# Gates, branch products and output projection in token form, and three of the gates' four column blocks from seven block products

## The chip, the cores and the metric

One core of a Trainium2 chip runs the whole kernel in one launch. The metric is the device time of that launch in microseconds, the median of several runs. All matrix products are done on TensorE in float32r, a float32 format in which one product of full accuracy is made from three passes: each operand is split into a high part and a remainder, and high by high, high by remainder and remainder by high are summed.

## What is computed

A decoder block for 256 tokens and 2048 channels: an mLSTM branch and an attention branch side by side, merged by sigmoid gates, an output projection with a residual, and then a squared-ReLU MLP with a residual. What the change touches is the middle of it:

```python
mq, mk, mv, mo, mi, mf, aq, ak, av, g_m, g_a = split_cols(rmsnorm(x) @ w_in)
h_m = mlstm(...) * sigmoid(mo)          # 256 x 1024
h_a = attention(...)                    # 256 x 1024
y_m, y_a = h_m @ w_branch_m, h_a @ w_branch_a           # 256 x 2048 each
merged = sigmoid(g_m) * y_m + sigmoid(g_a) * y_a        # g_m, g_a: 256 x 2048 each
x = x + rmsnorm(merged @ w_out)         # w_out: 2048 x 2048
u = square(relu(rmsnorm(x) @ w_up))
x = x + rmsnorm(u @ w_down)
```

## The kernel before, in words

Weights come from HBM in units of 1 MB (128 partitions by 2048 numbers), through three `raw` buffers, on the queue of SyncE (SP). `split` (line 157) turns each unit into high parts (`whi`, a cast on ScalarE, line 169) and remainders (`wlo`, a subtraction on VectorE, line 170), in pieces of 1024 columns with four buffers of each, so about one unit is being used while the next is made. The list `steps` holds for each unit what is loaded, the matmuls and what follows them; the main loop at the end loads and splits step i and then issues matmuls and follow-up of step i-1. A planner then orders each engine's instructions by a model of the time, with the program's order as priority, so it can pull later steps forward; only instructions marked `keep_in_program_order` keep their places.

There are four ways to do the matmuls of a unit. In the feature form (`mm_feat`, lines 188 and 189) the weights are the stationary operand and the 256 tokens stream past: for each of 16 blocks one pass of 512 columns (both parts of the activations) and one of 256. `mm_feat_one` (lines 215 to 217) does the same with three passes of 256. In the token form (`mm_tok`, lines 200 to 205) the activations are stationary and 512 columns of weights stream past: 24 passes of 512 columns for a unit. `mm_factor` (lines 226 to 232) is the token form for 128 tokens: 12 passes of 512 columns.

The order before: the values and mLSTM gate inputs (`av`), the attention heads with `q`, `k` and `mv`, then the mLSTM heads (`mq`, `mk`) with lighter units between them (`mv`, `mo`, the first gate units), then for each of 16 feature blocks c a branch step `br` and the gate steps `gm`, `ga` of block c + 4, then 16 units of the output projection (`wo`), then the MLP. The gates (32 units), `mo` (8), the branches (16) and 15 of the 16 `wo` units are in feature form. Their results come out feature by token; `both` (lines 236 to 241) adds the two halves of the accumulator on ScalarE and VectorE. `mlstm_out` gates and stores the last step of an mLSTM head. After the last `wo` unit (in the form of `mm_feat_one`) `last_mix` forms the norm's factor, `residual` makes the new x and its two parts, and the first up-projection step works on four units at once. `open_mlp` transposes x back into token order on TensorE (line 745).

The MLP already multiplies by seven block products in place of eight: `factors` and `group` make sums of blocks of activations and weights, and a group of seven products goes through `mm_factor`, between steps of the up-projection. Two of the seven weight blocks per group come from adding on VectorE (lines 856, 862 and 878, over 2048 columns) and one from a DMA that adds to what is in its destination (line 871, issued on GpSimd's queue, POOL).

## Time and profile before

| | us |
|---|---|
| median of 3 runs | 1439.17 (1438.96 to 1439.21) |
| the profiled execution's own time | 1440.65 |
| its span, first to last instruction | 1438.9 |
| TensorE matmul (PE) busy in it | 1415.9 |
| VectorE (DVE) busy | 1148.0 |
| ScalarE (ACT) busy | 816.2 |
| mean granted clock of TensorE | 0.998 |

The profiled execution took 1.48 us longer than the median; 1.75 us of its time lie outside its span. Busy time of PE counts a matmul from its start to its modelled end, and consecutive matmuls overlap, so how fast TensorE goes is read from the distance between starts, not from the busy time or the length of one.

### The profile page before, as it was taken

To read this page: it belongs to the slowest core of one execution; us is meant where nothing else is said; L and a number is where in the kernel's file an instruction comes from. 1 tells how busy PE (TensorE), PEld (TensorE's weight loads), DVE (VectorE), ACT (ScalarE), POOL (GpSimd) and SP (SyncE) were. 2 spreads that over 40 slices of the span, in tenths; PEclk is the share of its full clock that TensorE was granted. 3 is DMA by queue.
4 is the path that set the end of the run, shared out by engine and by line. 5 is a ranking of instruction groups with operands and counts; after the bars stand their busy time and mean duration, and the time that the engine had idled before them with its cause. 6 is when DMAs were issued, how large, how long until landed. Compare 5 with 4: busy or idle time off the path is not lost.

```text
span 1438.9 us, 21795 instructions
## 1 busy us (share of the span) xinstructions
PE 1415.9 (98%) x8578; PEld 1253.8 (87%) x8578; DVE 1148.0 (80%) x1607; ACT 816.2 (57%) x1200; POOL 14.5 (1%) x26
## 2 busy tenths in 40 slices
PE   9999999999999999999999999999999999999997
PEld 7888888888888888888899989989889898888975
DVE  7777766776676666665687899898999989999985
ACT  7655465565555444455656565564655655565561
POOL 0000000000000000000000000000000000000000
PEclk9999999999999999999999999999999999999999
DMA  8644444444445545555627665657646667665651
GB/s 258 218 176 176 174 165 161 175 174 176 176 176 182 200 177 195 184 183 197 236 76 247 236 216 179 253 197 263 226 151 242 219 217 239 212 205 193 237 202 59
DMA packets 44167, 281.65 MB, mean 196 GB/s; under 512 B 5024, under 2 KB 7328, under 8 KB 11424
## 3 DMA queue, kind: packets, MB, share of 16 engines
q1 hardware_dynamic: 41904, 265.57, 49.6%
q0 software_dynamic: 2016, 14.68, 5.5%
q8 instruction: 67, 1.10, 0.3%
q14 instruction: 36, 0.29, 0.1%
q10 hardware_dynamic: 144, 0.01, 0.0%
HBM read 278.14 MB, written 2.10 MB: 195 GB/s over the span
## 4 chain that ended last, share of the span: by engine, by line
PE 85%; DVE 11%; issue 2%; ACT 1%; DMA 1%; SPq 0%; DVEq 0%; ACTq 0%
PE acc L188 27%; PE acc L189 14%; PE acc L217 7%; PE acc L215 7%; PE acc L216 7%; DVE wlo L170 6%; PE acc L232 5%; PE acc L226 5%; PE acc L230 5%; PE acc L200 2%; PE acc L205 2%; PE acc L204 2%; DVE xs L774 1%; DVE rawl L862 1%; ACT whi L169 1%
## 5 line engine op out<-in xcount | busy, mean ns | idle before, releaser
L169 ACT CAST whi<-raw 128x1024 fp32r<-128x1024 f32 (+2 forms) x420 | 425.3, 1017 | 420.1 <-PE acc L188 179.1
L170 DVE TENSOR_TENSOR wlo<-raw,whi 128x1024 fp32r<-128x1024 f32 (+2 forms) x420 | 495.0, 1181 | 208.4 <-ACT whi L169 198.0
L188 PE MATMUL acc<-xw,whi 128*128 128x512 f32 x1152 | 408.9, 395 | 0.0
L189 PE MATMUL acc<-xw,wlo 128*128 128x256 f32 x1152 | 328.6, 285 | 0.0
L217 PE MATMUL acc<-hw,wlo 128*128 128x256 f32 x992 | 279.9, 283 | 4.9 <-DVE wlo L170 4.9
L216 PE MATMUL acc<-hw,whi 128*128 128x256 f32 x992 | 279.2, 282 | 0.0
L215 PE MATMUL acc<-hw,whi 128*128 128x256 f32 x992 | 277.7, 282 | 0.0
L188 PEld LDWEIGHTS acc<-xw,whi 128*128 128x128 f32 x1152 | 216.4, 188 | 50.3 <-issue 2.1
L169 ACT CAST whi<-rawl 128x1024 fp32r<-128x1024 f32 x168 | 173.5, 1048 | 116.8 <-PE acc L216 52.2
L189 PEld LDWEIGHTS acc<-xw,wlo 128*128 128x128 f32 x1152 | 216.7, 188 | 0.9
L170 DVE TENSOR_TENSOR wlo<-rawl,whi 128x1024 fp32r<-128x1024 f32 x168 | 201.8, 1218 | 8.4 <-ACT whi L169 6.5
L217 PEld LDWEIGHTS acc<-hw,wlo 128*128 128x128 f32 x992 | 186.9, 188 | 9.9 <-DVE wlo L170 7.3
L215 PEld LDWEIGHTS acc<-hw,whi 128*128 128x128 f32 x992 | 186.0, 188 | 4.6 <-DVE t L757 0.2
L216 PEld LDWEIGHTS acc<-hw,whi 128*128 128x128 f32 x992 | 186.8, 188 | 2.0
L226 PE MATMUL acc<-whi,xs 128*128 128x512 f32 x440 | 174.8, 397 | 2.9 <-ACT whi L169 2.9
L232 PE MATMUL acc<-wlo,xs 128*128 128x512 f32 x440 | 172.4, 397 | 1.8 <-DVE wlo L170 1.8
L230 PE MATMUL acc<-whi,xs 128*128 128x512 f32 x440 | 173.7, 395 | 0.0
L232 PEld LDWEIGHTS acc<-wlo,xs 128*128 128x128 f32 x440 | 82.6, 188 | 21.0 <-DVE wlo L170 4.5
L226 PEld LDWEIGHTS acc<-whi,xs 128*128 128x128 f32 x440 | 82.7, 188 | 20.7 <-ACT whi L169 6.0
L230 PEld LDWEIGHTS acc<-whi,xs 128*128 128x128 f32 x440 | 82.7, 188 | 18.1
L188 PE MATMUL acc<-mg,whi 128*128 128x512 f32 x240 | 84.2, 393 | 0.0
L189 PE MATMUL acc<-mg,wlo 128*128 128x256 f32 x240 | 67.7, 283 | 0.0
(258 smaller groups left out, 1622.1 us busy)
## 6 DMA issues: line engine op xcount, KB each, us to landing
raw<-in_wi_dram SPq DMA_DIRECT2D x96, 1024.0 KB, 4.8
raw<-in_wu_dram SPq DMA_DIRECT2D x64, 1024.0 KB, 6.2
rawl<-in_wd_dram SPq DMA_DIRECT2D x42, 1024.0 KB, 7.8
raw<-in_wd_dram SPq DMA_DIRECT2D x22, 1024.0 KB, 4.9
raw<-in_wo_dram SPq DMA_DIRECT2D x16, 1024.0 KB, 4.8
rawl<-in_wd_dram POOLq DMA_DIRECT2D x14, 1024.0 KB, 10.7
raw<-in_wa_dram SPq DMA_DIRECT2D x8, 520.0 KB, 4.6
raw<-in_wa_dram SPq DMA_DIRECT2D x16, 256.0 KB, 4.7
```

Source lines behind the costliest of these rows:

```text
L169: S.copy(out=hi[:, s], in_=r)
L170: V.tensor_tensor(out=lo[:, s], in0=r, in1=hi[:, s].bitcast(F32), op=ALU.subtract)
L188: PE.matmul(out=accs[i][:, 0:2 * T], lhsT=hi, rhs=m, start=k == 0, stop=False)
L189: PE.matmul(out=accs[i][:, 0:T], lhsT=lo, rhs=m[:, 0, :], start=False, stop=k == nk - 1)
L200: first = PE.matmul(out=acc, lhsT=m[:, 0, ts], rhs=hi, start=start and k == 0, stop=False)
L204: PE.matmul(out=acc, lhsT=m[:, 1, ts], rhs=hi, start=False, stop=False)
L215: PE.matmul(out=acc, lhsT=hi, rhs=m[:, 0, :], start=k == 0, stop=False)
L216: PE.matmul(out=acc, lhsT=hi, rhs=m[:, 1, :], start=False, stop=False)
L217: PE.matmul(out=acc, lhsT=lo, rhs=m[:, 0, :], start=False, stop=k == KT - 1)
L226: first = PE.matmul(out=acc, lhsT=f[:, k, 0], rhs=hi, start=start and k == 0, stop=False, skip_group_check=more)
L230: PE.matmul(out=acc, lhsT=f[:, k, 1], rhs=hi, start=False, stop=False, skip_group_check=more)
L232: PE.matmul(out=acc, lhsT=f[:, k, 0], rhs=lo, start=False, stop=stop and k == 3, skip_group_check=more)
```

## The change

The gates, `mo`, the branch products and the output projection go from feature form to token form. Of the gates' four blocks of 512 columns, the first is done plainly in token form. For each of the other three, the product of 2 x 2 blocks (rows: the two halves of the tokens; inner: the two halves of the 2048 channels; columns: the `ga` and the `gm` block) is made from seven products, each of two steps of `mm_factor`, 14 steps. Four sums of blocks of the activations are made once (`x_scale` and `x_sums` in place in x during the attention heads, and split in `open_gates`), the sums of weight blocks per column block: t by an adding DMA and two additions on VectorE, z by a load and an adding DMA. Per column block 12 units are fetched in place of 8, four of them by adding DMAs on POOL's queue. `mixed` lays plain steps (the last plain gate, the branches) between the 14. Gate results are taken from PSUM by one tanh (plain) or by a few copies and additions (seven products). `merged` transposes the merged activations on TensorE, 32 transposes of 128 columns. The output projection ends in two halves of 128 tokens, and `residual(h)` works on one half at a time, with transposes of the new x; the transposes of `open_mlp` and the matmuls of the squares of x are gone. x is not kept: it is loaded again (`x1_load`, 3 MB with the norm's weights) after the first `wo` unit. The first step of the up-projection has two units in place of four. Buffers move: x, the blocks t and two of the MLP's weight blocks share two places (`k8`), several others share six (`g4`), and `rawl` has two buffers in place of four.

```diff
-    light = [("mv", 1, u) for u in range(4)] + [("mo", c) for c in range(8)]
-    light += [("gm", 0), ("ga", 0), ("gm", 1), ("ga", 1)]
+    light = [("mv", 1, u) for u in range(4)] + [("mo", b, u) for b in range(2) for u in range(4)]
     for h in range(MH):
         for j, n in enumerate(("mq", "mq", "mk", "mk")):
-            o += [(n, 2 * h + j % 2), light[4 * h + j]]
-    o += [("gm", 2), ("ga", 2), ("gm", 3), ("ga", 3)]
-    for c in range(KT):
-        o.append(("br", c))
...
+            o.append((n, 2 * h + j % 2))
+            if j < 3:
+                o.append(light.pop(0))
...
+    def open_gates():
+        pb.close()
+        f = pool["f"] = pb.enter_context(tc.tile_pool(name="pg", bufs=1))
+        for name, src in (("q5", a22), ("q7", a21), ("p6", a11), ("q3", a12)) if SGATES else ():
+            t = fx[name] = f.tile([P, 8, 2, P], F32R, name="fac", tag="fac", bufs=4)
+            S.copy(out=t[:, :, 0], in_=src)
+            V.tensor_tensor(out=t[:, :, 1], in0=src, in1=t[:, :, 0].bitcast(F32),
+                            op=ALU.subtract)
...
+        def load_z(u):
+            r["z", u] = pool["f"].tile([P, 2048], F32, name="z", tag="z", bufs=1)
+            nc.sync.dma_start(out=r["z", u], in_=w(1, 0, u))
+            nc.gpsimd.dma_start(out=r["z", u], in_=w(1, 1, u), accum_op=ALU.add)
...
+        def w_p1(u):
+            t = r["t", u] = k8("t")
+            nc.sync.dma_start(out=t, in_=w(0, 0, u))
+            parts = split(t)
+            nc.gpsimd.dma_start(out=t, in_=w(1, 0, u), accum_op=ALU.add)
+            if u == 0:
+                load_z(0)
+            return parts
+        def w_p6(u):
+            r["22"] = load(w(1, 1, u))
+            if u == 0:
+                load_z(1)
+            add(r["t", u], r["22"])
+            return split(r["t", u])
+        def w_p2(u):
+            raw = load(w(0, 1, u))
+            parts = split(raw)
+            add(r["t", u], raw)
+            return parts
...
+        return [step(n, u) for n, u in (
+            ("p1", 0), ("p1", 1), ("q5", 0), ("q7", 0), ("p6", 0), ("q3", 0), ("q5", 1),
+            ("p6", 1), ("q3", 1), ("q7", 1), ("p2", 0), ("q4", 0), ("p2", 1), ("q4", 1))]
...
+    gate_steps(0, "m")
+    i = len(steps)
+    for k, f in ((i - 3, lambda: mlstm_out(3, heads.pop(3))), (i - 2, open_gates)):
+        src, mm, post = steps[k]
+        steps[k] = src, mm, lambda post=post, f=f: (post(), f())
+    both_gates(1, (gate_steps, 0, "a"))
+    both_gates(2, (branch_steps, 0, "a"), (branch_steps, 0, "m"), (branch_steps, 1, "a"))
+    both_gates(3, (branch_steps, 1, "m"), (branch_steps, 2, "a"), (branch_steps, 2, "m"))
+    then(lambda: [merged(c) for c in range(3)])
...
+        def mm(units):
+            late["hw"] = pa.tile([P, KT, 2, T], F32R, name="hw", tag="xw")
+            late["acc"] = tok_acc["o", 3]
+            for h in range(2):
+                for i in range(2):
+                    mm_tok(late["acc"], units[i], mgmov, 8 + 4 * i, False, i == 1, halves=(h,))
+                if h == 0:
+                    residual(0)
+        def post():
+            keep_warm(8)
+            residual(1)
+            open_mlp()
```

## Rows read from the trace of the kernel before

**Rows 1.** The page: busy time of TensorE, and the chain that ended last, by engine.
```profile
PE 1415.9 (98%) x8578; PEld 1253.8 (87%) x8578; DVE 1148.0 (80%) x1607; ACT 816.2 (57%) x1200; POOL 14.5 (1%) x26
PE 85%; DVE 11%; issue 2%; ACT 1%; DMA 1%; SPq 0%; DVEq 0%; ACTq 0%
```
**Rows 2.** Stretches: length, busy us of PE PEld DVE ACT POOL; clock, DMA share, GB/s.
```profile
440.00:680.00 240.00, 240.00 (x1369) 210.31 (x1368) 156.57 (x226) 122.77 (x194) 0.00 (x0) 1.00 0.51 187
943.50:1030.50 87.00, 85.60 (x553) 77.03 (x552) 81.97 (x84) 51.33 (x60) 1.71 (x2) 1.00 0.62 217
```
**Rows 3.** PE's timeline (start, us, what, [idle before]): 16 blocks in feature form.
```profile
300.10 0.40 PE L188 MATMUL acc<-xw,whi 128*128 128x512 f32 x1
...
305.72 0.39 PE L188 MATMUL acc<-xw,whi 128*128 128x512 f32 x1
```
**Rows 4.** Timeline of PE: 24 passes in token form, first and what follows them.
```profile
198.87 0.40 PE L200 MATMUL acc<-whi,xw 128*128 128x512 f32 x1
...
204.45 0.39 PE L188 MATMUL acc<-xw,whi 128*128 128x512 f32 x1
```
**Rows 5.** Timeline of PE: 38 passes of block products, then 48 of 256 columns.
```profile
1025.64 0.40 PE L226 MATMUL acc<-whi,xs 128*128 128x512 f32 x1
...
1034.28 0.39 PE L232 MATMUL acc<-wlo,xs 128*128 128x512 f32 x1
...
1000.09 0.28 PE L215 MATMUL acc<-hw,whi 128*128 128x256 f32 x1
...
1005.79 0.40 PE L226 MATMUL acc<-whi,xs 128*128 128x512 f32 x1
```
**Rows 6.** Timeline of DVE in the MLP and at the residual: back-to-back instructions.
```profile
944.55 1.22 DVE L170 TENSOR_TENSOR wlo<-raw,whi 128x1024 fp32r<-128x1024 f32 x1
945.68 0.68 DVE L846 TENSOR_TENSOR y<-y,acc 128x512 f32<-128x512 f32 x1
946.28 0.68 DVE L789 TENSOR_TENSOR s_b<-s_a,u 128x512 f32<-128x512 f32 x1
...
959.98 2.28 DVE L862 TENSOR_TENSOR rawl<-rawl 128x2048 f32<-128x2048 f32 x1
962.18 0.68 DVE L846 TENSOR_TENSOR y<-y,acc 128x512 f32<-128x512 f32 x1
...
722.46 0.48 DVE L710 SCALAR_TENSOR_TENSOR hw<-x,sm_in,hw 128x256 fp32r<-128x256 f32 x1
```
**Rows 7.** Timeline of PE and DVE: end of `wo`, first up, transposes, the tail.
```profile
715.82 0.28 PE L217 MATMUL acc<-mg,wlo 128*128 128x256 f32 x1
...
722.77 0.48 PE L215 MATMUL acc<-hw,whi 128*128 128x256 f32 x2
...
754.57 1.47 PE L745 MATMUL sm<-ident,x 128*128 128x128 f32 x12
...
1429.02 0.40 PE L232 MATMUL acc<-wlo,xs 128*128 128x512 f32 x1
...
1432.26 2.08 DVE L979 SCALAR_TENSOR_TENSOR x<-y,f_r,x 128x512 f32<-128x512 f32 x3
```
**Rows 8.** DMA: queues of the page, landing of adding DMAs, their issue, plain loads.
```profile
q1 hardware_dynamic: 41904, 265.57, 49.6%
q0 software_dynamic: 2016, 14.68, 5.5%
...
DMA to landing us min/median/max: 8.2/10.7/14.0
...
1025.94 0.85 POOL L871 DMA_DIRECT2D rawl<-in_wd_dram  x1 [43.08 <-DVE rawl L856]
...
raw<-in_wi_dram SPq DMA_DIRECT2D x96, 1024.0 KB, 4.8
```
**Rows 9.** Timeline of DVE: the last mLSTM head, first step after its keys and last.
```profile
372.30 0.75 DVE L240 TENSOR_TENSOR t<-acc,t 128x256 f32<-128x256 f32 x2
...
408.59 0.41 DVE L246 SCALAR_TENSOR_TENSOR hm<-t,hm 128x256 fp32r<-128x256 f32 x1
```

465 lines of the change are left out of this document (281 added, 184 removed).

## Prediction

> **What bounds the kernel now.** I read the page first: TensorE is busy in 98% of the span, and the chain that ended last runs through it for 85%, with VectorE next at 11% [rows 1]. The reader is to see that this is a TensorE kernel, and that busy time can't tell how much of it is waste. So next I looked at stretches: in 240 us of gates and branches PE is busy all the time at granted clock 1.00, with VectorE busy for 157 us of 240; in one cycle of the MLP VectorE is busy for 82 of 87 us and PE has its first idle time [rows 2]. The gates stage therefore has one limit, the rate at which passes go through TensorE, with VectorE as the next engine in line; the MLP shows what happens when VectorE is nearly full.
>
> The rate comes from starts. A unit in feature form takes 305.72 - 300.10 = 5.62 us [rows 3]; in token form 24 passes take 204.45 - 198.87 = 5.58 us [rows 4]; 37 pitches of block products take 8.64 us, 0.2335 us a pass, and a unit in three passes of 256 columns takes 5.70 us [rows 5]. Per column the four forms agree within 2.2%, so a pass saved is time saved, while a change of form is worth nearly nothing. The chip's notes point the other way here, in two sentences that nothing below needs. The Trainium skill (TensorE: Matmul & The Clock Gate, "Back-to-back issue gap") gives a sustained 131 ns for a pass of 512 columns and 81 ns for one of 128, which would make wide passes much cheaper per column and the token form a gain by itself; the rows have 232 to 234 ns for 512 columns and 119 ns for 256, proportional to columns within 2%, so by the trace there is no such gain.
>
> **The change part by part.**
>
> *Seven products for eight.* Three column blocks, each 8 units of 5.62 us before (44.96 us) and 14 steps of 12 passes after: 168 x 0.2335 = 39.23 us. That is 5.73 us each, **-17.2 us**, on the engine that sets the end.
>
> *Token form of the rest.* 8 gate units, 8 of `mo`, 16 of the branches and 15 of `wo` save 0.04 us each, and the last `wo` unit goes from 5.70 to 5.58: **-2.0 us**.
>
> *Transposes of the merged activations.* They are new: 32 at 0.109 us, from 12 in 1.31 us (the first start to the last one's end, less the first one's fill of 0.16) [rows 7], **+3.5 us**. The gaps that they could fill are counted below.
>
> *End of `wo` to first up-projection.* Before, the last pass of `wo` starts at 715.82 and takes its 0.12, and the first up pass starts at 722.77: 6.8 us without product; then 32 transposes, 3.5 us: 10.3 us. After, count from the end of the first half's 24 passes; the second half's last 5.6 us. The norm's factor needs 2.8 us, as in the tail where the last pass ends at 1429.42 and the first use of the factor starts at 1432.26 [rows 7]. Then VectorE has 4 updates of 512 columns (pitch 0.60) and 16 remainders of 128 columns. The trace has those only at 256 columns, where one lasts 0.48, pitch 0.40 with the overlap of 0.08 that the additions show; halving the columns takes off at most half and at least nothing; remainder and addition of 256 and 512 columns last 0.48 and 0.68, so 128 columns are about 0.10 to 0.13, and I take 0.27 [rows 6]: 2.4 + 4.3 = 6.7 us, done at 9.5. The second half's factor is there by 5.6 + 2.8 = 8.4, so VectorE sets it: one update, four transposes, a cast and a remainder more (0.60 + 0.44 + 0.5 + 0.1, the cast by the row of the 256-column remainder beside it) and the first up pass starts at 11.1. PE lacks 11.1 - 5.6 = 5.5 us, in which 20 of the 32 transposes of the new x lie; 12 follow, 1.3 us. So 6.8 against 10.3: **-3.5 us**. Its ends: 0 (every remainder at 0.40 adds 2, and the planner delays the second factor by one MLP-like queue), and -6 (the first up passes start as the 6.7 us queue of the second half begins, with transposes all hidden). I take the middle since both ends need something the rows don't show. After the start VectorE makes four k in 0.60 + 4 x 0.27 = 1.7 us and two units use four k in 24 x 0.119 = 2.9 us, so PE leads from there; before, with four units, it was close to even.
>
> The sum of these is **-19.2 us**. What could take it back is stalls, which the trace of before doesn't show for this stage; I bound them.
>
> *VectorE in the seven-product stretches.* A 1024-column remainder costs 1.13 us of VectorE, an addition of 512 columns 0.60, of 2048 columns 2.20 [rows 6]. Per column block: 28 x 1.13 + 4 x 2.20 + 6 x 0.60 = 44.0 us, against 39.2 of PE; alone, that is over. The plain units laid between have 2.26 us of VectorE in 5.58 of PE. Block 1 with 4 units: 53.1 of 61.6 us; blocks 2 and 3 with 6 units and 8 or 10 branch additions: 62.4 or 63.6 of 72.7. So 86 to 87%, less than the MLP's 94%, where a cycle of 14 block steps and 8 units should take 168 x 0.2335 + 8 x 5.70 = 84.8 us and takes 87.0 [rows 2, 5]: 2.2 us lost. That row is nearest, and bounds this at 0 to 2.2 us a block. ScalarE loses work, since one tanh takes the place of `both`.
>
> *The adding DMAs.* Per block four, against two in a whole MLP cycle with 43 us between them [rows 8]. One engine-share count: plain 265.57 MB in 49.6% of the span, so 2.8 us for a unit of 1.05 MB over all 16 engines; adding 14.68 MB in 5.5%, 5.65 us for a unit. Block 1 with its plain units: 12 x 2.8 + 4 x 5.65 = 56 of 61.6 us; blocks 2 and 3: 62 of 72.7. No average limit, but queues. The first adding DMA goes into t as soon as p1's split has read it, about when p1's first step starts. q5 follows after two block steps and a plain unit, 2 x 2.80 + 5.58 = 11.2 us later, and its first cast has to be done by then (1.05 us): cover 10.1 us. Landing takes 8.2 to 14.0 us, 10.7 in the median [rows 8]: a stall of 0 to 3.9 us, 0.6 in the median. The second, into z, has one step more, 12.9 us, but if it is served behind the first it lands 5.65 us later, 16.4 us: 3.4 us late in the median, 0 to 6.7 at the ends. Behind q5 and q7 on PE are p6 and q3; q3's weights come from a plain load, so the planner can put it or a plain unit first. New waits also hold queues: on POOL z's adding DMA stands behind t's, which waits for p1's split, and q7 waits for it; on SP the second z load waits for q7's split of the first, and behind it stand the raw loads of the next plain unit, which has two raw buffers ahead of it as cover. Together with VectorE I take 1.5 us a block, nearer to the MLP row because the planner has ordered that trace with the same means: **+4.5 us** (0 to 20).
>
> *Start of the first block.* The block sums of x lie in the two places that t needs, and their split in `open_gates` waits for the memory of the mLSTM's tiles, so for head 3. In the trace its last step ends 36.7 us after the first step that follows its keys [rows 9]. After it: three splits of 1.13 us, a load of 4.8 us [rows 8] and a cast, 46 us in all. Independent work behind the keys: four plain gate units, 22.3 us, and four more of `ga` that the planner may pull forward, 44.6 in all. So the hole is 46 - 44.6 = 1.4 us if they are pulled, and up to 18 (the tiles' chain made 5 us shorter by fewer VectorE steps, nothing pulled). PE in the gates stage had no idle time under this planner [rows 2], so I take **+2 us** (0 to 18).
>
> *Loads of x again.* 3 units more among 16 `wo` units on SP's queue, 8.4 us of DMA in 89 us that are half empty (share 0.51 [rows 2]). With three raw buffers, 11 us ahead, it hides; **+1 us** (0 to 4). The MLP's buffers: the blocks that change places are reused in the same order as before, so each waits for what it waited for; nothing, and 2.2 us a cycle more if one of them doesn't. `x_scale` and `x_sums` (16 casts, 4 subtractions) hide in the attention heads, where VectorE and ScalarE have the same free time as in the gates.
>
> Sum: -19.2 + 7.5 = **-11.7 us**, from the profiled execution's 1440.65 to 1428.95. That run was 1.48 above the median, so the timed runs should give **1427.5 us**.
>
> **The rivals.**
> *No stall.* If adding DMAs land in 8.2 us and the planner packs the stage as it did before, only the -19.2 stays: 1420 us. For it: the full PE of rows 2. Against it: DMA work per us doubles in kind. Beside it stands a rule, which nothing else rests on: the Trainium skill (DMA: Bandwidth & Descriptors, "Anatomy of one DMA") puts such a DMA at 2.0 us plus bytes over 436 GB/s, an estimate of 4.4 us for a unit, and by that the covers would always be enough; the trace's shortest is 8.2, so the trace does not agree.
> *The first block starts late.* The same gain, but the hole at head 3 is 10 us in place of 2: 1435.5 us; at 18 us, 1443. For it: `open_gates` comes behind a chain of 36.7 us whose PE steps wait for whole units. Against it: 22 us of `ga` that depend on none of it.
> *Slower: adding DMAs in pairs.* If t's and z's adding DMAs and the plain loads beside them slow each other, q5 and q7 wait in every block, three times. It decides at a landing of z of about 19.5 us: cover 12.9 plus (19.2 + 2.9 - 3) / 3 = 6.4 us a block is 0.2% slower than before. At 10 us a block the time is 1439.17 - 19.2 + 3 + 30 = 1453 us. For it: 14.0 us has been seen with one alone, and 14.0 + 5.65 is just there. Against it: median plus 5.65 is 16.4, and the planner has other steps.
> *The token form pays by itself*, if passes of 512 columns were cheaper in this stage than in rows 4: each 1% of 47 units is 2.6 us. Nothing in the rows speaks for it; it would take the time below 1417.
>
> **How the numbers follow.** Forecast (1421 to 1433): 0.55. First block late: 0.20, of which 0.08 end within 0.2% of before. Slower by adding DMAs: 0.12. No stall: 0.11. Token form: 0.02. 0.2%, 2.9 us, is about what a measurement of this kernel can tell from no change. So faster 0.55 + 0.12 + 0.11 + 0.02 = 0.80, same 0.08, slower 0.12. The range goes from 1417 (the -19.2 with the -6 end of the boundary) to 1439 (forecast with a first hole of 13.5); outside it lie the slower case, the token form and a few hundredths of the late start.
>
> **What would show it.** Block products in the gates at a pitch of 0.2335 and 504 of them; PE idle before q5 and q7, released by a DMA, of some 3 us a block (none: no stall; 8 or more: the slower case); PE idle ahead of the first p1 released by t's load or the factors (2 us; more than 6: late start); about 5.5 us between the last `wo` pass and the first up pass, much of it transposes; MLP cycles of 87 us as before. I am wrong if token passes or block products have another pitch in this stage, if VectorE ends the waits of whole blocks though it has 13% free, or if the MLP's cycle grows by its new buffers.

## The result, and the profile of the changed kernel

The changed kernel takes **1510.52 us** (median of four runs, 1506.37 to 1513.21) against 1439.19: 1.0492 times as long, 95% interval 1.0464 to 1.0520. The forecast was 1427.5 us, 12 us faster than before; it is 71 us slower than before, far above the range. The profiled execution took 1508.53 us with a span of 1506.7 us, 67.8 more than before.

The page of the changed kernel first: busy time, the granted clock in 40 slices, and the chain that ended last.
```profile
PE 1428.2 (95%) x7892; PEld 1226.1 (81%) x7892; DVE 1182.1 (78%) x1506; ACT 829.1 (55%) x1132; POOL 24.7 (2%) x38
PEclk9999999998899999999989999999999999999999
PE 79%; DVE 11%; DMA 5%; ACT 2%; issue 2%; SPq 0%; DVEq 0%; ACTq 0%
```
Beside [rows 1] the reader is to see two things. TensorE made 686 matmuls fewer and yet was busy for 12 us more: it ran slower at times, which is what the 8s in the clock's row say. And the chain has DMA in it for 5% where it had 1%.

Where the time went is read from TensorE's timeline: the start of the first (or last) matmul of each stage. Worked out so, in us:

| stretch | before | after | difference |
|---|---|---|---|
| start to the last pass of 260 columns | 54.6 | 62.2 | +7.6 |
| to the first output projection (heads, gates, branches) | 571.4 | 598.5 | +27.1 |
| to the first up-projection | 96.8 | 112.9 | +16.1 |
| to the first down-projection | 52.6 | 48.2 | -4.4 |
| seven cycles of the MLP | 608.2 | 630.0 | +21.8 |
| rest | 55.2 | 54.9 | -0.3 |

Four stages lost, in four different kinds of work, so no single wait explains it. TensorE's waits, longest first (what waited, for whom: us in total, times, longest), and four stretches in the columns of [rows 2]: the hole behind the last conv unit, two blocks of seven products with their plain units, one cycle of the MLP.
```profile
PE acc L232 <- ACT whi L175: 29.3, 12, 7.0
PE sm L891 <- DVE x L886: 12.9, 4, 3.9
PE acc L238 <- DVE wlo L176: 6.6, 13, 2.1
PE sm L488 <- DVE qkm L468: 3.8, 1, 3.8
```
```profile
359.30:403.00 43.70, 30.66 (x122) 23.44 (x121) 20.20 (x43) 17.43 (x29) 1.00 (x1) 0.86 0.41 143
403.00:474.90 71.90, 67.56 (x265) 51.41 (x265) 53.90 (x46) 39.30 (x42) 3.41 (x4) 0.94 0.80 230
474.90:557.20 82.30, 77.00 (x313) 60.41 (x314) 66.99 (x60) 46.46 (x49) 3.40 (x4) 0.96 0.78 250
997.10:1087.60 90.50, 87.50 (x554) 78.89 (x553) 82.25 (x84) 51.07 (x60) 1.70 (x2) 0.98 0.61 209
```
Where [rows 2] have PE busy for all of 240 us at clock 1.00, it is now idle for 13.0, 4.3 and 5.3 us in the first three stretches, at clocks of 0.86 to 0.96; a cycle that took 87.00 us takes 90.50, half of the growth in idle time and half in slower passes (85.60 us busy before, 87.50 now).

What was foreseen rightly: the products themselves. There are 504 passes in the three blocks, and 15 of them start from 581.09 to 584.35, a pitch of 0.233 us as in [rows 5]:
```profile
581.09 0.39 PE L232 MATMUL acc<-whi,fac 128*128 128x512 f32 x1
...
584.35 0.39 PE L238 MATMUL acc<-wlo,fac 128*128 128x512 f32 x1
```

### The profile page after: what moved, and what is told of

It is laid out like the page before. It is cut to its first block, busy times and chain, and to the rows that moved or that the text cites. A ratio compares the mean times of both kernels' runs of the same rounds, so it can differ in the third digit from the quotient of the medians.

```text
span 1506.7 us, 20304 instructions
## 1 busy us (share of the span) xinstructions
PE 1428.2 (95%) x7892; PEld 1226.1 (81%) x7892; DVE 1182.1 (78%) x1506; ACT 829.1 (55%) x1132; POOL 24.7 (2%) x38
## 4 chain that ended last, share of the span: by engine, by line
PE 79%; DVE 11%; DMA 5%; ACT 2%; issue 2%; SPq 0%; DVEq 0%; ACTq 0%
PE acc L223 8%; PE acc L221 8%; PE acc L222 8%; PE acc L194 8%; PE acc L238 7%; PE acc L232 7%; PE acc L236 7%; DVE wlo L176 5%; PE acc L211 4%; PE acc L206 4%; PE acc L210 4%; PE acc L195 4%; PE sm L206 2%; PE sm L210 2%; PE sm L211 2%
## 5 line engine op out<-in xcount | busy, mean ns | idle before, releaser
L175 ACT CAST whi<-raw 128x1024 fp32r<-128x1024 f32 (+2 forms) x396 | 399.0, 1014 | 346.9 <-PE acc L222 109.3
L176 DVE TENSOR_TENSOR wlo<-raw,whi 128x1024 fp32r<-128x1024 f32 (+2 forms) x396 | 463.2, 1179 | 149.6 <-ACT whi L175 144.7
L194 PE MATMUL acc<-xw,whi 128*128 128x512 f32 x512 | 183.5, 397 | 0.0
L195 PE MATMUL acc<-xw,wlo 128*128 128x256 f32 x512 | 146.5, 286 | 0.0
L175 ACT CAST whi<-bt 128x1024 fp32r<-128x1024 f32 x84 | 86.0, 1046 | 83.2 <-PE acc L222 40.6
L194 PEld LDWEIGHTS acc<-xw,whi 128*128 128x128 f32 x512 | 96.2, 188 | 22.9 <-issue 1.9
L176 DVE TENSOR_TENSOR wlo<-bt,whi 128x1024 fp32r<-128x1024 f32 x84 | 101.2, 1220 | 13.4 <-ACT whi L175 13.3
L195 PEld LDWEIGHTS acc<-xw,wlo 128*128 128x128 f32 x512 | 96.3, 188 | 1.3 <-issue 0.2
L175 ACT CAST whi<-rawl 128x1024 fp32r<-128x1024 f32 x56 | 58.6, 1047 | 47.5 <-PE acc L222 34.6
L176 DVE TENSOR_TENSOR wlo<-t,whi 128x1024 fp32r<-128x1024 f32 x48 | 57.7, 1222 | 33.9 <-ACT whi L175 32.1
```

Of the source, the lines that this page charges most:

```text
L175: S.copy(out=hi[:, s], in_=r)
L176: V.tensor_tensor(out=lo[:, s], in0=r, in1=hi[:, s].bitcast(F32), op=ALU.subtract)
L194: PE.matmul(out=accs[i][:, 0:2 * T], lhsT=hi, rhs=m, start=k == 0, stop=False)
L195: PE.matmul(out=accs[i][:, 0:T], lhsT=lo, rhs=m[:, 0, :], start=False, stop=k == nk - 1)
```

## The experiments

Each run is one kernel beside a run of the kernel before on the same chip, which took 1439.1 to 1440.7 us. Changes are against the changed kernel unless said. All stretches are read as in the table above. The changed kernel's own runs lie 6.8 us apart, so where a run differs from it by less, its stretch is read and not its time. Stretches vary too: the one to the first output projection takes 598.5 to 602.7 us in five kernels that have it unchanged (the changed kernel, e2_sum_buffers, e3_passes_first, e5_four_and_four, e6_rotation). The kernels e1 to e16 were run once each.

### The token form without the seven products

```diff
-SGATES = (1, 2, 3)
+SGATES = ()
```


> The token form alone: all four column blocks of the gates from eight block products, nothing else changed against the kernel after (so no scaled copy of x, no sums of x, no adding DMAs outside the MLP). Theory A (the 71 us are several separate losses, each made by the order or the buffers of one stage): the start goes back by about 7 us (its new work on ScalarE is gone), the stretch from the last attend matmul to the first output projection goes from 442 to 415 to 425 us (as before the change: the same products without the new chains), while the output projection keeps its 105 us and the MLP's cycles their 90.5 us; in all 1475 to 1485 us. Theory B (the adding DMAs and what they do to the other transfers and to the clock are the one cause): everything goes back, output projection and cycles too, 1435 to 1445 us.

**1495.4 us**, above both forecasts, and nearer to theory A's 1475 to 1485. The start loses 3.4 us instead of 7.6; the stretch to the first output projection takes 588.5 us, still 17.1 more than before; the output projection (112.2) and the MLP (631.5) keep all that they lost. So 56 of the 71 us come without the seven products, from orders and buffers that stay in this run, and the products, meant to save 17.2 us, cost 15.1 (1510.5 - 1495.4).

### The MLP's buffers

```diff
-            r["12"], r["t"] = k8("b12"), k8("bt")
+            r["12"], r["t"] = long_raw(), k8("bt")
...
-            r["22"] = long_raw()
+            r["22"] = k8("b22")
```


> In the MLP only the partners of two buffer pairs are exchanged: the sum of weights shares its pair with the block b22, and b12 shares with b21, so that the next group's first sum needn't wait until the sum of this group has been split for q4. Theory A (the cycle's 3.4 us is this one wait: the sum comes late, behind the splits of q4 and the factors on VectorE): the idle time of about 3 us once a cycle before the first matmul of a q5 goes, cycles of 87.0 to 87.7 us instead of 90.5, 1487 to 1493 us. Rival (the cycle is long because the factors and u share buffers, or because the clock is lower): cycles stay at 90 us or more, 1505 to 1512 us.

**1504.7 us**; seven cycles take 622.2 us instead of 630.0: neither theory's number, a third of the loss. The changed kernel's VectorE and ScalarE at the start of a cycle show what the sum (`w_t1`) waits for:
```profile
995.10 1.22 DVE L176 TENSOR_TENSOR wlo<-bt,whi 128x1024 fp32r<-128x1024 f32 x1
...
1000.31 2.28 DVE L1038 TENSOR_TENSOR bt<-raw,b 128x2048 f32<-128x2048 f32 x1
```
```profile
1002.70 2.00 ACT L175 CAST whi<-bt 128x1024 fp32r<-128x1024 f32 x2 [4.14 <-DVE bt L1038]
```
One buffer holds the sum for q5, p6 and q4 in turn, so three of a group's seven weight blocks come from additions on VectorE (lines 856, 862 and 878 before). The next group's sum (`bt<-raw,b`) may be written only when the last remainder of this group's sum has been read (995.10 + 1.22). By then the factors stand ahead of it in VectorE's queue, so it comes at 1000.31, its splits at 1002.70, and the first pass that needs them starts at 1003.80, 3.16 us after the pass before it. In the kernel before, the four buffers are one pool, and the sum came ahead of the last four remainders of its group (938.09 to 943.41), q3's and q4's:
```profile
935.88 2.29 DVE L856 TENSOR_TENSOR rawl<-raw,rawl 128x2048 f32<-128x2048 f32 x1
```
So the buffer that it took had been free by then; by the order of the splits it was b12's. In e2_sum_buffers the sum shares with b22, which only q3's split frees (read from the code, not from a row). The next run gives it b12's place:
```diff
+            if not ring:
+                ring.extend((k8("b"), k8("b"), long_raw(), long_raw()))
+            r["12"], r["t"], r["22"], r["21"] = ring[0], ring[1], ring[3], ring[2]
+            ring[:3] = ring[2], ring[0], ring[1]
```


> The MLP's four weight buffers rotate as they did before the change: b22 keeps one, and b12, the sum and b21 go around three, so that the next sum takes the buffer of b12 (free after q7's split). Theory A (the whole growth of the cycle is where the next sum may be written, and e2_sum_buffers gave back only part since its sum still waits for q3's split): cycles of 86.9 to 87.4 us, 608 to 612 us for seven instead of 629.9 (622.2 in e2_sum_buffers), 1488 to 1492 us in all. Rival (what e2_sum_buffers left, 2.4 us a cycle, comes from the factors' and u's shared buffers or the two buffers for r): 620 to 624 us for seven, 1501 to 1506 us.

**1488.5 us**, as theory A said; seven cycles take 606.4 us, a little under its 608. One cycle of it:
```profile
996.70:1083.50 86.80, 85.53 (x554) 77.05 (x552) 82.05 (x84) 51.38 (x59) 1.71 (x2) 1.00 0.64 218
```
Same work on every engine as in the cycle of the changed kernel above, 3.7 us shorter, and the granted clock is at 1.00 again although nothing was done for it. The stretch behind the changed kernel's wait shows that the two go together:
```profile
1003.80:1008.00 4.20, 4.20 (x23) 4.11 (x24) 4.20 (x6) 2.03 (x3) 0.16 (x1) 0.66 0.88 257
```
There the granted clock is 0.66, and passes of 256 columns start 0.21 us apart from 1005.19 to 1008.60, where they start 0.12 apart before and after.

### The end of the output projection

The second half's passes are pinned, and a pin holds an instruction behind the one recorded before it on its engine. That was the last transpose of the residual's first half. TensorE did what the code says:
```profile
749.72 1.97 PE L891 MATMUL sm<-ident,x 128*128 128x128 f32 x8 [3.92 <-DVE x L886]
...
758.50 1.11 PE L891 MATMUL sm<-ident,x 128*128 128x128 f32 x4 [2.55 <-DVE x L886]
759.27 0.78 PE L206 MATMUL acc<-whi,mg 128*128 128x512 f32 x1
...
760.27 0.63 PE L211 MATMUL acc<-wlo,mg 128*128 128x512 f32 x1
760.70 0.63 PE L206 MATMUL acc<-whi,mg 128*128 128x512 f32 x1
```
24 passes that were ready waited behind 16 transposes, and the first nine of them then started 0.43 us apart or more instead of 0.233, at a granted clock of 0.69 from 759.3 to 765.0.
```diff
                     mm_tok(late["acc"], units[i], ... halves=(h,))
-                if h == 0:
-                    residual(0)
         def post():
+            residual(0)
             keep_warm(8)
```


> Both halves' passes of the last output column are recorded before the residual of the first half (the pin of the second half's passes then no longer stands behind the residual's transposes), and the early activation that loads the square root's table takes the first sum of squares as its input. Theory A: TensorE no longer idles between the two halves (13.9 us from 745.4 to 759.3 before it), the first residual runs beside the second half's 5.6 us; first up comes 9 to 13 us earlier, 1497 to 1502 us in all. Rival (the chain of the residual sets the end of this stage whatever TensorE does ahead of it): the idle time only moves behind the second half, first up comes 0 to 4 us earlier, 1506 to 1511 us.

**1505.9 us**; to the first up 109.2 instead of 112.9: the rival was right, the idle time moved. (This run also has the square root's table late, which belongs to the start.) The residual's chain sets the end. Its rows in this run, on ScalarE and VectorE:
```profile
760.25 0.37 ACT L896 ACTIVATE hw<-sm,sm_in 128x128 fp32r<-128x128 f32 x1 [0.42 <-DVE hw L897]
761.04 0.37 ACT L896 ACTIVATE hw<-sm,sm_in 128x128 fp32r<-128x128 f32 x1 [0.42 <-DVE hw L897]
```
```profile
759.87 0.35 DVE L897 SCALAR_TENSOR_TENSOR hw<-sm,sm_in,hw 128x128 fp32r<-128x128 f32 x1 [0.51 <-ACT hw L896]
760.65 0.35 DVE L897 SCALAR_TENSOR_TENSOR hw<-sm,sm_in,hw 128x128 fp32r<-128x128 f32 x1 [0.43 <-ACT hw L896]
```
A high part by ScalarE waits for the low part of the column before it by VectorE, and the other way round: 0.78 us a column. Both read one bank of PSUM, and the program lets one engine at a time at a bank. The Trainium skill (PSUM — Partial Sum Buffer, "PSUM bank collisions raise a hardware error") gives the reason: the chip doesn't arbitrate two engines in a bank, so they have to be kept apart by semaphores; the rows agree with that, and no run here tried it without.
```diff
...
-                S.activation(out=hw[:, k, 0, hs], in_=p, func=AF.Copy, scale=g)
-                pin(V.scalar_tensor_tensor(out=hw[:, k, 1, hs], ...))
+            for k, p, g in parts:
+                S.activation(out=hw[:, k, 0, hs], in_=p, func=AF.Copy, scale=g)
+            for k, p, g in parts:
+                pin(V.scalar_tensor_tensor(out=hw[:, k, 1, hs], ...))
```


> As e3_passes_first, and in the residual ScalarE writes the four high parts of a bank of transposed columns before VectorE writes the four low parts, instead of one and one in turn. Theory A (the end of the output projection is set by the residual's chain, in which ScalarE and VectorE take turns on one bank: 0.78 us a column, 16 columns a half, two halves): a bank's four columns take about 2.3 us instead of 3.7 to 4.6, and the next bank's high parts go beside this one's low parts; from the first output projection to the first up 97 to 104 us instead of 112.8 (109.2 in e3_passes_first), 1494 to 1500 us in all. Rival (the chain is bound by its start, sums, square root and Newton steps behind the splits of the up weights in VectorE's queue, and the turns lie beside that): 107 to 110 us, 1503 to 1507 us.

**1502.2 us**, 106.9 to the first up: just under the rival's 107 to 110, and far from theory A's 97 to 104. A bank now takes 1.14 us on ScalarE, but the second half starts late:
```profile
761.43 1.14 ACT L897 ACTIVATE hw<-sm,sm_in 128x128 fp32r<-128x128 f32 x4 [0.45 <-PE sm L891]
762.45 0.65 ACT L852 ACTIVATE q<-x 128x512 f32<-128x512 f32 x1
...
763.22 0.60 ACT L852 ACTIVATE q<-acc 128x512 f32<-128x512 f32 x1
763.80 1.14 ACT L897 ACTIVATE hw<-sm,sm_in 128x128 fp32r<-128x128 f32 x4
```
The second half's sum of squares (`q<-acc`), whose last pass had started at 752.3, stands in ScalarE's queue behind the first half's casts until 763.22. e9_token_mended takes it out of there.

### The start

In the first 62.2 us ScalarE makes, beside what it made before:
```profile
L618 ACT ACTIVATE x<-x,pre_in 128x256 f32<-128x256 f32 x16 | 7.6, 501 | 0.0
L866 ACT ACT_TABLE_LOAD x1 | 1.3, 1283 | 0.0
```
```diff
+        if n == 0:
+            late["pre"] = ...
+            V.scalar_tensor_tensor(out=late["pre"], in0=ha[:, 0, 0, 0:KT].bitcast(F32), scalar=0.0,
+                                   in1=pre_in, op0=ALU.mult, op1=ALU.add)
...
-            ... scale=pre_in[:, k:k + 1])
+            ... scale=late["pre"][:, k:k + 1])
...
```


> The scaled copy of x takes its column from a copy of the pre-norm weights that is made only after the first attention head, and its four parts and the sums stand one head later. Theory A (the start lost 7.6 us because the planner drew these 16 activations into the stretch in which ScalarE is the bound): the last matmul of the first token units goes from 62.2 to 56 to 59 us, and nothing else changes: 1504 to 1507 us. Rival (the start is late because of x's loads in two buffers or because of the square root's table): 61 to 64 us and 1508 to 1512 us.

**1506.8 us**; start 58.6 us, as theory A said. The stretch behind it takes 602.7 us, at the upper end of its spread, so the time itself shows less than the start. The 16 activations were drawn ahead into the stretch where ScalarE is the bound. The square root's table is a second such piece: its early activation read `rhalf`, ready at once. e1_plain_gates and e9_token_mended have no scaled copy, and with that activation at its late place the start falls from 58.0 to 54.7 us; with both mended it takes 53.2 to 55.3 us, as before the change.

### The hole ahead of the first block

The counterpart of [rows 9] on TensorE:
```profile
362.62 0.67 PE L488 MATMUL sm<-qkm 128*128 128x256 f32 x2 [1.57 <-DVE ml_e L483]
367.14 1.22 PE L488 MATMUL sm<-qkm 128*128 128x256 f32 x2 [3.84 <-DVE qkm L468]
...
403.00 0.80 PE L232 MATMUL acc<-whi,xw 128*128 128x512 f32 x1 [6.97 <-ACT whi L175]
```
Matmuls of the last head stand in TensorE's queue ahead of gate units that are ready (1.57, 3.84 and 0.65 us of waiting), and the first block's weights come 6.97 us after the last plain unit.
```diff
     gate_steps(0, "m")
+    gate_steps(0, "a")
...
-    both_gates(1, (gate_steps, 0, "a"))
-    both_gates(2, (branch_steps, 0, "a"), (branch_steps, 0, "m"), (branch_steps, 1, "a"))
...
+    both_gates(1, (branch_steps, 0, "a"), (branch_steps, 0, "m"))
+    both_gates(2, (branch_steps, 1, "a"), (branch_steps, 1, "m"))
...
```
(and the last head is recorded behind the first of these gate units).

> The gates' second plain column (four units, 22.4 us) stands ahead of the first block of seven products instead of among it, two branch columns take its place there, and the last mLSTM head is recorded two units later so that its matmuls don't stand in TensorE's queue ahead of units that are ready. Theory A (the hole of about 14 us around the first block is the head's chain, the factors' splits and the load behind them, for which only four units were cover): the idle time between the last conv unit and the first block's end of loads goes from about 14 to 0 to 4 us, 1496 to 1502 us. Rival (the loads that wait for x's buffers are late in any order because the queue holds them): the gap ahead of the first block stays at 7 us, 1506 to 1511 us.

**1501.0 us**, as theory A said: 588.1 us to the first output projection, 10.4 less than the changed kernel. Not all of the hole is gone, though. The wait ahead of the first block is, but one wait in the last head's own chain is left, where theory A had 0 to 4 us in all:
```profile
PE sm L538 <- DVE t L532: 6.6, 1, 6.6
```
The kernels from e8_all_mended on spread that head over more plain units.

### All of it together

For e8_all_mended the units laid among a block's products also go to one place:
```diff
-        n, done = len(others), 0
...
+        steps.extend(first[:2] + others + first[2:])
```


> All of it together: rotation of the MLP's buffers, both halves' passes first and four columns in a row in the residual, the scaled copy late, the square root's table late, the gates' second column and one branch column ahead of the first block of seven products, the last mLSTM head's steps spread over these units, and in each block the branch units behind the two first products. Theory A (separate losses that add up): start 4 to 6 us, head and blocks 10 to 20, output projection 9 to 15, MLP 18 to 22, less than 1510.5 by 45 to 60: 1450 to 1465 us, with single waits of 1 to 3 us left in the blocks. Rival (the adding DMAs keep the blocks late whatever stands around them): from the last attend matmul to the first output projection no less than 430 us and 1470 to 1480 us in all.

**1467.3 us**, between the two: start and MLP as before the change or better (54.9, 606.3), but 595.0 us to the first output projection. What is left is in the blocks. So three things are separated: the token form with everything mended, the place of the plain units, and the adding DMAs. In e9_token_mended and all that follow but e16_changed_no_adding, both halves' sums are formed ahead of the residual's columns, which then alternate between the halves:
```diff
+        for h in range(2):
+            mix_evac(3, h, late["acc"][h])
+            ...
+            rsqrt_act(r[h], v, 1)
+        keep_warm(16)
+        for e, h in [(e, h) for e in range(5) for h in range(2)]:
```


> The token form alone (all gates from eight block products), mended: the MLP's rotation, the square root's table late, the last mLSTM head's steps spread over eight plain units, and a residual that forms both halves' sums first and then goes bank by bank, half by half, four high parts before four low parts. Theory A (the losses outside the blocks of seven are orders and buffers, and go one by one): start 55 to 58 us; from the last conv unit to the first output projection 278 to 283 us (291.5 in e1_plain_gates); from there to the first up 96 to 101 us (105.2 to 112.8 before); MLP as in e6_rotation; 1440 to 1448 us in all, level with the kernel before. Rival (the token form itself is slower at these places): 1452 us or more.

**1442.9 us**: 576.8 us to the first output projection, 97.6 to the first up, 607.2 for seven cycles, each as theory A said. The sum of squares is no longer behind the casts:
```profile
722.91 0.59 ACT L855 ACTIVATE q<-acc 128x512 f32<-128x512 f32 x1
```
One more thing differs there. `keep_warm` is a run of filler matmuls (products of ones whose result nobody reads). The changed kernel has 8 of them, behind the second half's passes; this edit has 16, right behind the last pass:
```profile
721.93 3.73 PE L150 MATMUL sm<-ones 128*128 128x128 f32 x32
```
From 721.9 to 729.1 the granted clock is 1.00; in the changed kernel it is 0.64 from 745.4 to 759.3 and 0.76 from 770 to 776. What the fillers give apart from the order, no run shows.

The token form alone, mended, is 3.8 us slower than the kernel before (1439.1 beside it).

```diff
-SGATES = ()
+SGATES = (1, 2, 3)
```
(against e9_token_mended, with the late copy of e7_scale_late)

> As e9_token_mended with the three blocks of seven products, the scaled copy late, and the plain units spread evenly among a block's units as the change had them (e8_all_mended had them behind the two first products). Theory A (inside a block VectorE is the bound: 14 splits at 2.4 us, four adds of 2.28 us and the sums of accumulators make some 50 us beside 39 us of products, so plain units must lie among them): the loss of the blocks falls from some 36 us in e8_all_mended to 15 to 25, from the last conv unit to the first output projection 277 to 287 us instead of 298, 1440 to 1452 us in all. Rival (the loads of t at a block's start and the adding DMAs, which no order of plain units makes earlier): 292 us or more for that stretch, 1453 to 1460 us.

**1458.7 us**, 594.6 us to the first output projection, the same as with the plain units in a lump (595.0): the rival was right, where the plain units lie is not what the blocks wait for. (The loads and the adding DMAs, which the rival names, are separated in the next runs.)

```diff
-            nc.gpsimd.dma_start(out=r["z", u], in_=w(1, 1, u), accum_op=ALU.add)
...
-            nc.gpsimd.dma_start(out=t, in_=w(1, 0, u), accum_op=ALU.add)
```


> As e10_spread without the adding DMAs of the blocks: t and z are loaded and not added to, so 12 transfers and their sums are left out of the gates. Theory A (VectorE is the bound in a block, the adding DMAs are mostly hidden): 0 to 5 us less than e10_spread. Theory B (the adding DMAs, their 10 us landing and the bandwidth that they take from the plain loads, are what the blocks wait for): 10 to 20 us less.

**1430.7 us**, 28.0 less: theory B, and more than its 10 to 20. The first two blocks with and without the adding DMAs:
```profile
410.90:480.60 69.70, 56.74 (x218) 42.79 (x216) 52.24 (x48) 34.31 (x37) 3.41 (x4) 0.93 0.76 221
480.60:552.40 71.80, 66.04 (x264) 51.05 (x265) 58.58 (x52) 40.56 (x43) 3.40 (x4) 0.95 0.77 236
```
```profile
411.90:467.20 55.30, 52.78 (x218) 41.43 (x217) 51.90 (x48) 35.32 (x37) 0.00 (x0) 0.97 0.48 178
467.20:532.20 65.00, 62.16 (x265) 49.45 (x264) 57.97 (x53) 40.04 (x42) 0.00 (x0) 1.00 0.56 209
```
VectorE has the same 52 and 58 us of work in both, in 69.7 and 71.8 us or in 55.3 and 65.0; the DMA share falls from 0.76 and 0.77 to 0.48 and 0.56, and the clock rises.

Where TensorE waits in e10_spread's blocks is in its trace, and it is not where the prediction's rival "adding DMAs in pairs" has it. None of its waits of over 0.4 us is for the sum z, whose adding DMA lands last. It waits long for t's adding DMA once (5.75 us ahead of the first q5), and otherwise mostly in a block's first two steps (p1), whose plain load of t is late, and in the second step of p6. There VectorE's sum, in the second and the third block, waits for a plain load:
```profile
518.56 2.29 DVE L717 TENSOR_TENSOR t<-t,raw 128x2048 f32<-128x2048 f32 x1 [3.58 <-DMA raw<-in_wg_dram]
```
This load was issued at 506.90, 1.6 us after an adding DMA into z, and landed with it, after 11.6 us. Of the 48 plain loads of gate and branch weights in this run, 22 had an adding DMA beside them and took 9.0 us in the median; the other 26 took 4.8.

```diff
-            t = r["t", u] = k8("t")
+            parts = split(load(w(0, 0, u)))
+            t = r["t", u] = k8("t")
             nc.sync.dma_start(out=t, in_=w(0, 0, u))
-            parts = split(t)
...
```


> As e10_spread, but the first product's weights are loaded a second time into the plain weight buffers, so that a block's first two units don't wait until the previous block has freed the buffers of t; the branch column that stood ahead of the first block goes back among its units. Theory A' (the wait at a block's start is t's buffers: freed by q4's splits, then a load of 5 to 9 us): the gaps of 2 to 4 us ahead of p1 go, 3 to 10 us less than e10_spread. Rival (the DMA engines are near full in a block, 0.64 to 0.84 of their time in e8_all_mended, and six more loads of 1 MB make all others later): the same or up to 5 us more than e10_spread.

**1461.2 us**, 2.5 more: the rival. The second block gains 3.2 us, the third loses 1.6, and in the first, with the branch column back among its units, one wait of 12.2 us comes ahead of the first q5. The blocks' plain loads land in 5.9 us where e10_spread has 5.0: what a buffer gains, the fuller DMA engines take.

### What an adding DMA costs

```diff
-            nc.gpsimd.dma_start(out=r["z", u], in_=w(1, 1, u), accum_op=ALU.add)
+            nc.gpsimd.dma_start(out=r["z", u], in_=w(1, 1, u))
...
-            nc.gpsimd.dma_start(out=t, in_=w(1, 0, u), accum_op=ALU.add)
+            nc.gpsimd.dma_start(out=t, in_=w(1, 0, u))
```


> As e10_spread, but the second transfer into t and z (same queue, same 1 MB, same place in the chain of load, second transfer, split) overwrites instead of adding, so the gates' sums lack one term. Theory C (the adding itself: its packets take twice the time on the DMA engines, so it lands late and holds the other transfers up): the second transfers land in 5 to 7 us instead of 10, and 12 to 25 us less than e10_spread. Theory D (the chain: a split that must wait for a second transfer from another queue, and 12 MB more to move, whatever it does on landing): 0 to 8 us less than e10_spread.

**1440.8 us**, 17.8 less than e10_spread: theory C. Landing times in the blocks (us, median of six), first of e10_spread, then of this run:
```profile
t<-in_wg_dram SPq DMA_DIRECT2D x6, 1024.0 KB, 9.2
z<-in_wg_dram POOLq DMA_DIRECT2D x6, 1024.0 KB, 12.5
t<-in_wg_dram POOLq DMA_DIRECT2D x6, 1024.0 KB, 10.1
```
```profile
t<-in_wg_dram SPq DMA_DIRECT2D x6, 1024.0 KB, 6.9
z<-in_wg_dram POOLq DMA_DIRECT2D x6, 1024.0 KB, 7.8
t<-in_wg_dram POOLq DMA_DIRECT2D x6, 1024.0 KB, 5.2
```
Same bytes, same queue, same place in the chain: without the adding they land in 7.8 and 5.2 us instead of 12.5 and 10.1, and the plain load of t beside them in 6.9 instead of 9.2. Of the 28 us, some 18 are the adding and some 10 the second transfer (single runs on two chips, where the kernel before took 1439.1 and 1440.7 us).

> The changed kernel itself without its 12 adding DMAs in the gates (their terms are left out of the sums), everything else as it is: what the adding DMAs cost there. If the cost is as in the mended kernel (28 us between e10_spread and e11_no_adding): 1478 to 1487 us. If the head's hole and the plain units hide part of it: 1488 to 1500 us. The start, the output projection and the MLP's cycles keep what they lose in every case.

**1491.0 us**: in the changed kernel as it is the adding DMAs cost 19.5 us, 16.9 of them in the stretch to the first output projection. That other waits hide the rest of the 28 us, as the second forecast has it, no run shows by itself.

Can another engine form the sums? In the next two runs w21 and w22 are loaded plainly and added by GpSimd (`G`) or by VectorE (`V`):
```diff
+            nc.sync.dma_start(out=z, in_=w(1, 0, u))
+            r["22", u] = load(w(1, 1, u))
+            G.tensor_tensor(out=t, in0=t, in1=z, op=ALU.add)
+            G.tensor_tensor(out=z, in0=z, in1=r["22", u], op=ALU.add)
```


> As e10_spread, but GpSimd forms the sums for t and z from plainly loaded blocks (w21 goes to z, is added to t, and w22, which has to be loaded for its own product, is added to z): 12 adding DMAs less, 12 sums on an engine that had nothing to do. Theory C: the blocks lose their 10 us landings, 10 to 25 us less than e10_spread, 1434 to 1449 us, if a sum of 128x2048 on GpSimd takes under some 5 us and doesn't slow VectorE. Rival (GpSimd and VectorE hold each other up, or the sums take 8 us and more): the same as e10_spread or more, 1457 to 1480 us, with longer splits on VectorE beside GpSimd's sums.

**1477.8 us**, 19.2 more: the rival. A sum on GpSimd takes 4.6 to 5.7 us, and VectorE's remainders stop while it lasts:
```profile
433.01 4.91 POOL L716 TENSOR_TENSOR t<-t,z 128x2048 f32<-128x2048 f32 x1 [12.96 <-DMA z<-in_wg_dram]
```
```profile
432.22 1.23 DVE L176 TENSOR_TENSOR wlo<-t,whi 128x1024 fp32r<-128x1024 f32 x1 [0.80 <-ACT whi L175]
434.08 4.92 DVE L176 TENSOR_TENSOR wlo<-raw,whi 128x1024 fp32r<-128x1024 f32 x1 [0.64 <-ACT whi L175]
```
```profile
L176 DVE TENSOR_TENSOR wlo<-t,whi x32: 1212/1218/5591, 411.5 to 559.7; 128x1024 fp32r<-128x1024 f32 x32
```
(minimum, median and maximum in ns). A remainder takes 1.22 us, and beside a sum 4.92: it ends 1.1 us after GpSimd does.

> As e14_gpsimd_sums with VectorE in GpSimd's place: 12 sums of 2.28 us, 27 us more work on VectorE in a stretch of some 300 us where it is at 0.75 to 0.83 in the blocks. Theory C with VectorE as the next bound: block windows at 0.9 or more on VectorE, 5 to 18 us less than e10_spread. Theory D or a full VectorE: the same or more.

**1452.5 us**, 6.2 less, as theory C with VectorE next. In the first block VectorE is now busy for 58.64 of 60.80 us (67.31 of 72.30 and 84.21 of 95.50 in the two after it):
```profile
412.60:473.40 60.80, 53.89 (x217) 40.98 (x216) 58.64 (x50) 34.01 (x37) 0.00 (x0) 0.97 0.43 156
```

### Fewer blocks, spread wider

If VectorE's sums are the cheapest and it is full in a dense block, the block has to be spread. Two column blocks from seven products, with ten plain units among the first (one branch column's half and the plain gates of block 2) and eight among the second:
```diff
...
+    mixed(seven_steps(1), (branch_steps, 0, "m"), (gate_steps, 2, "m"), (gate_steps, 2, "a"))
+    mixed(seven_steps(3), (branch_steps, 2, "a"), (branch_steps, 2, "m"), (branch_steps, 1, "a"),
+          (branch_steps, 1, "m"))
```


> Two column blocks from seven products (1 and 3), two from eight, the sums for t and z on VectorE as in e15_vector_sums, ten plain units among the first block's products and eight among the second's; otherwise as e10_spread. Theory (a block of seven pays 5.7 us of TensorE if the plain units around it give VectorE and the loads their time): against e9_token_mended's 1442.9 us twice 5.7 less, and 3 to 6 us more for the scaled copy, the factors and single waits: 1434 to 1440 us, level with the kernel before or up to 0.4% faster. Rival (the sums on VectorE still make waits in a block whatever is among it): 1443 to 1450 us.

**1431.9 us** (five runs, 1430.1 to 1433.1), 0.9944 times the kernel before, interval 0.9931 to 0.9956: 0.6% faster than the kernel before, which is little but clear of these runs' spread, and under the theory's 1434 to 1440. It is 11.0 less than e9_token_mended of the 11.5 that two blocks can give. Its two blocks, the second with what follows it up to the output projection:
```profile
410.90:506.10 95.20, 95.17 (x410) 76.75 (x409) 83.32 (x70) 54.15 (x57) 0.00 (x0) 1.00 0.56 201
506.10:619.00 112.90, 109.54 (x482) 88.19 (x481) 93.74 (x87) 60.73 (x67) 0.00 (x0) 1.00 0.52 188
```
TensorE is busy for 95.17 of 95.20 us at clock 1.00, VectorE for 83.32. Against e15_vector_sums two things have changed, the number of blocks and the plain units around each; no run separates them.

> As e17_two_blocks_vector, with the adding DMAs as the change has them. Theory C (an adding DMA costs what it takes of the DMA engines while plain loads run, 28 us for three dense blocks, and less where a block's products are spread over 85 to 95 us): 1436 to 1444 us. Rival (their cost is per DMA, 2.3 us each, however the block is spread): 8 x 2.3 = 18 us less 11.5 gained, 1449 to 1455 us.

**1437.6 us** (11 runs), 0.998 [0.9971, 0.9990]: theory C. That is 6.2 us above e9_token_mended less the full 11.5, so the eight adding DMAs cost at most 0.8 us each, where e10_spread against e11_no_adding has 2.3. Their landing (11.9 and 10.5 us) is no shorter; that there is more to cover it is the likely reason, argued and not shown. Beside e17_two_blocks_vector the loss is 5.6 us, and in the traces it lies in the first of the two stretches shown there (102.0 us against 95.2; the second takes 113.0 against 112.9).

## Why the prediction was wrong, point by point

**Seven products, -17.2.** Passes, pitch and saving per block were right. With nothing else in the way two blocks gave 11.0 of 11.5 us (e17_two_blocks_vector against e9_token_mended), and three gave 12.2 of 17.2 even with splits of x and x_scale to make (e11_no_adding).

**Token form -2.0, merged transposes +3.5.** In e9_token_mended 56 units change form ahead of the first output projection, which with the transposes should have made +1.3 us (3.5 - 56 x 0.04); it has +5.4 (576.8 against 571.4). A term mis-sized by 4 us, and the trace shows where. The transposes' products were sized rightly, but they don't run in one go: TensorE's only wait in that stretch stands among them, for VectorE's remainders of the merged activations, and the 6.2 us behind it run at clock 0.72:
```profile
PE sm L797 <- DVE mg L803: 2.3, 1, 2.3
```
```profile
605.80:612.00 6.20, 6.20 (x25) 4.79 (x26) 3.10 (x5) 1.79 (x3) 0.00 (x0) 0.72 0.48 169
```
That is 2.3 us of waiting and some 1.7 us of slower passes (0.28 x 6.2, an estimate from the clock). The forecast spoke of gaps that these transposes could fill; they made one.

**The adding DMAs and VectorE, +4.5 (0 to 20).** This is the step with the wrong mechanism: I held the MLP's 2.2 us a cycle to be the nearest row, where two adding DMAs have 43 us between them [rows 8], and priced the queueing of two as a matter of cover. In the changed kernel they cost 19.5 us, in the mended one 28, 9.3 a block. The rival "adding DMAs in pairs" with 10 us a block came nearest; I gave it 0.12. It names the plain loads beside them, but its size is partly luck: its arithmetic needs a landing of z after some 19.5 us and waits at q7, and z landed after 12.5 us in the median and 13.1 at most in e10_spread, with no wait of TensorE over 0.4 us for it. What the runs show in its place is that the plain loads beside an adding DMA are late (9.0 us in the median where the others take 4.8), so that steps wait which I had not counted as waiting for it, p1 and the second step of p6. That the DMA engines had 56 us of work in 61.6 I passed over as "no average limit". VectorE, which I counted at 86 to 87% there, was not it: the same work fits into 55 instead of 70 us.

**Start of the first block, +2 (0 to 18).** At the far end of its range: TensorE is idle for 13.0 us in the stretch of 43.7, and at clock 0.86 its passes lose some 4 more (0.14 of 30.7 us busy, an estimate). The chain itself was sized rightly (46 us forecast), the cover was not. I counted `ga` as pulled ahead, which was the planner's to do and wasn't done; and [rows 2], full in a stage without this chain, were no evidence for a stage with it. e4_cover_first got 10.4 us back by writing that order into the program.

**Loads of x again, +1 (0 to 4).** No run has this term by itself; with the loads in place the mended end of `wo` comes out as forecast, so it can't be large.

**End of `wo` to first up, -3.5 (0 to -6).** Wrong: +11.7 (16.1 more to the first up, 4.4 less behind it, where 32 transposes had stood). Single durations were right (four low parts in 1.12 us in e5_four_and_four, where I had 0.27 a column), the order was not. I let the second half's passes run beside the first half's chain, though `mm_tok` pins the passes of a single half (`halves=(h,)` in the diff), and let ScalarE and VectorE work on one bank side by side. With pin, turns and the second half's sum all mended, and with twice the fillers, it is -2.4 (97.6 + 49.4 against 96.8 + 52.6), near the forecast; the first alone gave 3.7 us of the 16, the first two 6.0.

**The MLP's buffers, "nothing".** Wrong by 21.8 us, the largest single loss of the changed kernel. I compared the order in which buffers are asked for, not the pools: in one pool of four the next sum had a buffer that was free in time, in two pairs it gets its own again. My alternative, 2.2 us a cycle, was short by a third (21.8 / 7 = 3.1); it had no term for the slower passes, which are half of the growth of the cycle shown. The sign named for this step ("if the MLP's cycle grows by its new buffers") is the one that came.

**`x_scale` hides in the attention heads.** Wrong: it ran ahead of them, where its inputs were ready and ScalarE was the bound; 3.6 us of the start (e7_scale_late).

The pieces add up: 22 from the MLP (e6_rotation), 10 from the hole (e4_cover_first), 14 from the boundary (e9_token_mended) and 7 from the start, taken from 1510.5, give 1457.5, and e10_spread, with these four mended, took 1458.7. The 28 us of the adding DMAs were measured from there and are no test of the sum; without them e11_no_adding, whose sums lack terms, takes 1430.7, some 3 us above the forecast.

## What to carry to other kernels

A change that saves passes on a full engine is judged by what the other engines and queues must do in the same stretch. For transfers an average below the limit is no answer: the forecast had 56 us of DMA work in 61.6, adding transfers at twice a plain one's share, and the stretch still lost. Ask which plain loads run beside an adding one, and what waits for them. Moving buffers from one pool into two, pinning an instruction, or making an input ready earlier are changes of order, and each cost 4 to 22 us here without a line of arithmetic being different. Read for each what it waits for, and what in a queue is then behind it.

## What the runs showed of the hardware

An adding DMA of 1 MB lands in 10 to 12.5 us beside plain loads (medians of t and z in e10_spread), an overwriting one from the same queue in 5 to 8 (e13_second_overwrites), and plain loads of 1 MB that run beside an adding one take 9.0 us in the median instead of 4.8. Leaving an adding DMA out gains 2.3 us in three dense blocks (28.0 / 12); with two blocks and more plain units it costs at most 0.8.

A wait of 2 to 3 us cost about twice its length in the two cases read here. In the MLP's cycle TensorE was idle for 1.6 us more (3.00 against 1.40 [rows 2]) and lost another 1.9 us to slower passes, those at clock 0.66 behind the wait; in e9_token_mended a single wait of 2.3 us was followed by 6.2 us at clock 0.72. Behind the idle time at the residual (13.9 us between the two halves' passes) passes of 512 columns started 0.43 us apart instead of 0.233, and passes of 256 in the MLP 0.21 instead of 0.12: nearly twice, as the two levels of 1.2 and 2.4 GHz have it. The kernel before has waits of 0.4 and 1.0 us in each MLP cycle and a granted clock of 1.00 there [rows 2].

While GpSimd's sum runs, VectorE's remainder does not. The Trainium skill (SBUF — State Buffer, "Who interferes with whom") says that a VectorE instruction with two inputs in SBUF contends with a GpSimd instruction that reads SBUF, as an exclusive lock; the rows at 433 and 434 us agree: 4.92 us for an instruction of 1.22. An addition with one input in PSUM (`a<-a,sm`, at 410.16 in the same trace) took its usual 0.69 us beside a sum.
